# Splitting a layer's mixing weights on two compute engines instead of with chained DMAs, and moving two tiles to other PSUM banks, in a two-layer hybrid encoder

## The chip, the core and the metric

The kernel runs on one core of a Trainium2 chip. The core has five engines that this text names: TensorE (PE, matmuls; its weight loads are PEld), VectorE (DVE), ScalarE (ACT), GpSimd (POOL) and SyncE (SP), which here only issues DMAs. Each engine works through its own queue in order, and waits on semaphores for the others. The metric is the device time of one execution in microseconds (us).

## The reference

Two layers of a bidirectional encoder over 512 tokens of width 1024, in float32. Each layer mixes the tokens with attention heads and a recurrent group side by side, and then applies a gated MLP:

```python
h = rmsnorm(x, g_mix[l])
z = h @ w_in[l]                                   # 1024 x 2560
q, k, v, x_rec, gate = split(z)                   # 512 each
att = neighbourhood_attention(q, k, v, rel_bias[l])       # 8 heads of 64, 8 x 16 window
xc = depthwise_conv(x_rec, ...)
rec = (rg_lru(xc, forward) + rg_lru(xc, backward)) * gelu(gate)
x = x + concat(rmsnorm(att), rmsnorm(rec)) @ w_out[l]     # the mixing part ends here
h = rmsnorm(x, g_ffn[l])
u_act, u_lin = split(h @ w_up[l])                 # 3072 each
x = x + (gelu(depthwise_conv(u_act)) * u_lin) @ w_down[l]
```

A last rmsnorm follows the second layer.

## The kernel before

Every float32 product is made of three matmuls (mm3): each operand is split into a rounded half hi and the remainder lo, and hi*hi + hi*lo + lo*hi are accumulated in PSUM. The activations lie transposed, 128 features by 512 tokens a tile.

The weights come in chunks of 128 x 1024 (eight blocks of 128 x 128; the gates of the recurrence have chunks of 128 x 512). weight_plan lists the chunks in the order of their use, and chunk hands out the next one; at that moment it calls split_to for the chunks up to three ahead and load_to for those up to six ahead. There are four hi and four lo buffers (p_hi, p_lo) and two raw buffers (p_raw). A chunk gets its halves in one of three ways:

- The common way (lines 171 to 184 and 204 to 213): SP loads the chunk into a raw buffer, ScalarE writes the rounded hi (L210), VectorE subtracts to get lo (L211). MLP and output weights go this way in both layers, and the first four chunks of each layer.
- By DMA (by_dma, L157; L175 and lines 194 to 204), in layer 0 for the query, key, value and gate columns of w_in and for the recurrence's gates, 20 chunks in all: GpSimd issues a DMA that casts the chunk straight into hi; ScalarE copies it negated into lo (L200, ahead of its other work by urgent(1)); then GpSimd issues a second DMA that reads the chunk again and adds it to lo (L201).
- Kept (kept, L217 to L234), for the same 20 chunks of layer 1: they are split during the MLP of layer 0 and stored in DRAM, and SP loads both halves (L172).

The mixing part of a layer follows the hand-written list MIX, which is the order of PE's work as the code is written. A scheduler then places the instructions of each engine's queue; work inside urgent() comes early. The steps that matter here, for heads in pairs (block i holds heads 2i and 2i + 1): q, k, v and g are the query, key, value and gate tiles i (24 matmuls each; "a" and "b" are their halves), t are the gates of the recurrence, c its convolution, u the value's transposes to tokens, S the scores of a head with their maximum and exponentials, T the transposes of its probabilities, P the products with the values. A block reads `k1a t1a k1b P1 t1b v1a e0 S2 v1b S3 g1a u1 c3 g1b T2 q2a q2b P2 T3`. The values exist as vh and vl (L611, L612); GpSimd copies shifted parts of them into edge (L616) for the products at the window's edge. The probabilities are split into pt tiles by ScalarE (L708) and VectorE (L709), the whole part first and the edge part second.

PSUM has eight banks: three in ps_mm, two in ps_s (scores), two in ps_pt (transposed probabilities), one in ps_o. The first projection of a layer (xr, columns 12 to 15) takes the three of ps_mm and ps_o; query and key tiles take ps_mm (L575, L584).

Of the kernel before, what the change touches and what calls it, by code (L numbers as in the profile page):

```python
# [10 lines left out]
F32R = mybir.dt.float32r  # L11
AF = mybir.ActivationFunctionType
ALU = mybir.AluOpType

P = 128
# [85 lines left out]
def encoder(ctx: ExitStack, tc: tile.TileContext, x_d, w_d, cols_d, bias_d, out_d):  # L101
    nc = tc.nc
    plan = weight_plan()
# [16 lines left out]
    p_lo = pool("p_lo", 4)  # L120
# [3 lines left out]
    ps_mm = pool("ps_mm", 3, PS)  # L124
    ps_s = pool("ps_s", 2, PS)
# [6 lines left out]
    def psum(pl, name):  # L132
        return pl.tile([P, T], F32, tag="ps", name=name)
# [6 lines left out]
    def f32(ap):  # L140
        return ap.bitcast(F32)

    def urgent(level=2):
        return tc.high_priority(offset=level * URGENT) if level else ExitStack()


    raws, highs, lows, halves, kept = {}, {}, {}, {}, {}
# [1 line left out]
    AHEAD_LOAD, AHEAD_SPLIT = 6, 3  # L149

    def pieces(i):
        return (slice(0, 1024),) if i else (slice(0, 512), slice(512, 1024))

    def width(i):
        return P * len(plan[i][2])

    def by_dma(i):  # L157

        w, _, bs = plan[i]
        return w == "gate" or w == "w_in" and bs[0][1] != 12  # L160

    def load_to(n):
        while state["load"] < min(n, len(plan)):
            i = state["load"]
            if by_dma(i):
                if i > state["use"] + 3:
                    return
                highs[i] = p_hi.tile([P, 1024], F32R, tag="hi", name=f"hi{i}")
                if i in kept:
                    lows[i] = p_lo.tile([P, 1024], F32R, tag="lo", name=f"lo{i}")  # L170
                    for n, t in enumerate((highs[i], lows[i])):
                        for h in range(width(i) // 512):  # L172
                            nc.sync.dma_start(f32(t[:, 512 * h:512 * h + 512]), kept[i][n, h])
                else:
                    nc.gpsimd.dma_start(highs[i][:, :width(i)], w_d[i][:, :width(i)])  # L175
                state["load"] += 1
                continue
            raws[i] = p_raw.tile([P, 1024], F32, tag="raw", name=f"raw{i}")
            for n, sl in enumerate(pieces(i)):
                nc.sync.dma_start(raws[i][:, sl], w_d[i][:, sl])  # L180
                if i == n == 0:
                    nc.sync.dma_start(x[0], x_d[0])
            state["load"] += 1

    def split_to(n):
        while state["split"] < min(n, len(plan)):
            i = state["split"]
            if by_dma(i) and i > state["use"] + 2:
                return
            load_to(i + 1)  # L190
            if i in kept:
                halves[i] = highs.pop(i), lows.pop(i)
                state["split"] += 1
                continue
            if i in highs:
                hi = highs.pop(i)
                lo = p_lo.tile([P, 1024], F32R, tag="lo", name=f"lo{i}")
                with urgent(1):
                    ws = slice(0, width(i))
                    nc.scalar.activation(lo[:, ws], f32(hi[:, ws]), AF.Copy, scale=-1.0)  # L200
                    nc.gpsimd.dma_start(lo[:, ws], w_d[i][:, ws], accum_op=ALU.add)  # L201
                halves[i] = (hi, lo)
                state["split"] += 1
                continue
            raw = raws.pop(i)
            hi = p_hi.tile([P, 1024], F32R, tag="hi", name=f"hi{i}")
            lo = p_lo.tile([P, 1024], F32R, tag="lo", name=f"lo{i}")
            with urgent(0):
                for sl in pieces(i):
                    nc.scalar.activation(hi[:, sl], raw[:, sl], AF.Copy)  # L210
                    nc.vector.tensor_tensor(out=lo[:, sl], in0=raw[:, sl], in1=f32(hi[:, sl]), op=ALU.subtract)  # L211
            halves[i] = (hi, lo)
            state["split"] += 1

    later = [i for i in range(len(plan)) if by_dma(i) and plan[i][1] == 1]

    def split_later():  # L217

# [273 lines left out]
    def layer(l, xn):  # L492
# [79 lines left out]
        qk = {}  # L572

        def query_tile(i):
            ps = psum(ps_mm, f"qps{l}{i}")  # L575
            yield from column_parts(ps, "w_in", l, i, xg, 4)
            with urgent():
                for n in range(2):
                    rows = slice(64 * n, 64 * n + 64)
                    nc.vector.tensor_tensor(out=in_group(q_pair[rows, :, n]), in0=by_group(ps)[rows],  # L580
                                            in1=by_group(rb)[rows], op=ALU.mult)

        def key_tile(i):
            ps = psum(ps_mm, f"kps{l}{i}")  # L584
            yield from column_parts(ps, "w_in", l, 4 + i, xg, 4)
            qk[4 + i] = big(p_h, "h", f"k{l}{i}")
            with urgent():
                nc.vector.scalar_tensor_tensor(out=qk[4 + i], in0=ps, scalar=0.125, in1=rb, op0=ALU.mult, op1=ALU.mult)
# [366 lines left out]
```

## Time and profile before

| | |
|---|---|
| runs shown | 1227.52 us median (three runs, lowest 1226.66, one of them 2701.48) |
| profiled execution | 1226.75 us, of which 1224.0 us lie between its first and its last instruction (span) |
| PE busy | 1198.3 us, 98% |
| VectorE busy | 736.7 us, 60% |
| ScalarE busy | 503.7 us, 41% |
| GpSimd busy | 123.7 us, 10% |
| DMA | 161.29 MB, 132 GB/s over the span |

The mixing part of layer 0 fills about the first 200 us, its MLP the time to about 610 us; then layer 1 does the same. The profile's engine times are shares of the span. A row of a timeline gives start and duration in us, engine, line, operation, output and inputs; the bracket at its end is the time that the engine stood idle before it, and what it waited for. Matmul rows overlap, as they are pipelined: their pace is read from the distances of their starts.

### The profile page before, as it was taken

The page shows a single profiled execution, that of the slowest core. Times are in us where ns is not written, and L with a number is a line of the kernel's source. Part 1 is how long each engine was busy: PE and PEld are TensorE (multiplying, and loading weights), DVE is VectorE, ACT ScalarE, POOL GpSimd, SP SyncE. Part 2 cuts the span into 40 slices and gives each one's busy share as a digit, 9 for nine tenths or more (in the row PEclk, how much of TensorE's full clock was granted, in tenths as well). Part 3 has the DMA queues.
Part 4 walks back from the last instruction along what each step waited for, and adds up shares of the span by engine and source line. Part 5 has one row for each costly group of instructions (what it writes and reads, how often), then busy time and mean ns, then how long its engine had stood idle before and what let it go on. Part 6 is the DMA issues. An engine that isn't in the chain of part 4 may idle for free.

```text
span 1224.0 us, 14611 instructions
## 1 busy us (share of the span) xinstructions
PE 1198.3 (98%) x5566; PEld 999.0 (82%) x5566; DVE 736.7 (60%) x1217; ACT 503.7 (41%) x741; POOL 123.7 (10%) x206
## 2 busy tenths in 40 slices
PE   9888999999999999999999999999999999999997
PEld 7777788888888888888888888888888888888886
DVE  6476684877653376662736777677556255555454
ACT  5566783544332144332416667443322212323220
POOL 3222210022220022210000100100000000000000
PEclk9999999999999999999999999999999999999999
DMA  8656632366663366653245443142232332322322
GB/s 270 142 133 124 140 104 70 103 206 213 229 217 99 102 216 224 215 171 103 92 132 191 141 148 104 38 136 90 100 104 88 101 103 86 104 93 96 103 69 69
DMA packets 53942, 161.29 MB, mean 132 GB/s; under 512 B 6768, under 2 KB 9968, under 8 KB 53872
## 3 DMA queue, kind: packets, MB, share of 16 engines
q1 hardware_dynamic: 39328, 113.17, 28.3%
q0 software_dynamic: 14400, 47.20, 14.1%
q8 instruction: 43, 0.70, 0.2%
q14 instruction: 27, 0.22, 0.1%
q10 hardware_dynamic: 144, 0.00, 0.0%
HBM read 139.37 MB, written 20.97 MB: 131 GB/s over the span
## 4 chain that ended last, share of the span: by engine, by line
PE 90%; DVE 4%; issue 3%; DMA 1%; POOL 1%; ACT 1%; POOLq 0%; DVEq 0%; ACTq 0%
PE dn L248 7%; PE dn L250 7%; PE dn L249 7%; PE pa L248 7%; PE pl L248 7%; PE pa L249 7%; PE pl L249 7%; PE pl L250 7%; PE pa L250 7%; PE out L250 2%; PE out L248 2%; PE out L249 2%; DMA hi<-in_w 1%; PE up L248 1%; PE up L250 1%
## 5 line engine op out<-in xcount | busy, mean ns | idle before, releaser
L210 ACT ACTIVATE hi<-raw 128x1024 fp32r<-128x1024 f32 (+1 forms) x169 | 178.3, 1055 | 388.3 <-PE dn L249 160.5
L211 DVE TENSOR_TENSOR lo<-raw,hi 128x1024 fp32r<-128x1024 f32 (+1 forms) x169 | 205.3, 1215 | 133.5 <-ACT hi L210 132.7
L818 DVE TENSOR_TENSOR ua<-pa,g_ffn_rb 128x512 f32<-128x512 f32 x44 | 30.4, 692 | 113.7 <-PE pa L250 113.7
L826 ACT ACTIVATE uc<-uc,cols 128x512 f32<-128x512 f32 x48 | 34.8, 724 | 115.9 <-DVE uc L824 115.9
L827 DVE TENSOR_TENSOR uc<-pl,uc 128x512 f32<-128x512 f32 x44 | 30.3, 689 | 44.6 <-PE pl L250 43.8
L466 POOL TENSOR_TENSOR fin_r<-fin_ms,expo 128x2 f32<-128x2 f32 x2 | 1.4, 697 | 377.7 <-DVE fin_ms L464 377.7
L795 DVE TENSOR_TENSOR dns<-dn,g_ffn_rb 128x512 f32<-128x512 f32 x30 | 20.5, 689 | 29.4 <-PE dn L250 29.4
L233 POOL DMA_DIRECT2D kept<-lhi x36 | 19.5, 543 | 177.8 <-ACT lhi L227 174.5
L824 DVE SCALAR_TENSOR_TENSOR uc<-ua,cols,uc 128x511 f32<-128x511 f32 x48 | 36.0, 750 | 1.5
L822 DVE SCALAR_TENSOR_TENSOR uc<-ua,cols,uc 128x511 f32<-128x511 f32 x48 | 35.7, 744 | 0.1
L200 ACT ACTIVATE lo<-hi 128x1024 fp32r<-128x1024 f32 (+1 forms) x20 | 19.4, 972 | 32.7 <-DMA hi<-in_w 24.6
L228 DVE TENSOR_TENSOR llo<-lraw,lhi 128x512 fp32r<-128x512 f32 x36 | 24.7, 687 | 10.7 <-ACT lhi L227 10.7
L682 ACT ACTIVATE prob<-prob,mx 128x192 f32<-128x192 f32 (+1 forms) x64 | 27.5, 430 | 1.1 <-DVE mx L680 0.9
L248 PE MATMUL out<-atth,hi 128*128 128x512 f32 x64 | 25.7, 402 | 0.0
L249 PE MATMUL out<-attl,hi 128*128 128x512 f32 x64 | 25.2, 394 | 0.0
L201 POOL DMA_DIRECT2D lo<-in_w x20 | 17.5, 877 | 75.8 <-ACT lo L200 75.8
L250 PE MATMUL out<-atth,lo 128*128 128x512 f32 x64 | 25.2, 393 | 0.0
L616 POOL CAST edge<-vh 64x384 fp32r<-64x384 f32 x16 | 10.1, 629 | 144.3 <-ACT vh L611 143.8
L233 POOL DMA_DIRECT2D kept<-llo x36 | 19.5, 543 | 48.9 <-DVE llo L228 46.3
L821 DVE TENSOR_SCALAR uc<-ua,cols 128x512 f32<-128x512 f32 x48 | 23.4, 487 | 1.6
L667 PE MATMUL s<-k,q_pair 128*128 128x192 f32 (+1 forms) x128 | 22.0, 314 | 2.4 <-DVE mx L675 2.4
L556 DVE SCALAR_TENSOR_TENSOR ti<-ti,xc 128x512 f32<-128x512 f32 x16 | 11.0, 689 | 21.9 <-ACT ti L548 21.9
(934 smaller groups left out, 3687.2 us busy)
## 6 DMA issues: line engine op xcount, KB each, us to landing
raw<-in_w SPq DMA_DIRECT2D x167, 512.0 KB, 3.5
lraw<-in_w POOLq DMA_DIRECT2D x36, 256.0 KB, 4.2
kept<-lhi POOLq DMA_DIRECT2D x36, 256.0 KB, 2.5
kept<-llo POOLq DMA_DIRECT2D x36, 256.0 KB, 3.0
hi<-kept SPq DMA_DIRECT2D x36, 256.0 KB, 2.8
lo<-kept SPq DMA_DIRECT2D x36, 256.0 KB, 4.0
hi<-in_w POOLq DMA_DIRECT2D x16, 512.0 KB, 5.4
lo<-in_w POOLq DMA_DIRECT2D x16, 512.0 KB, 5.6
```

The costliest lines, as they stand in the source:

```text
L210: nc.scalar.activation(hi[:, sl], raw[:, sl], AF.Copy)
L211: nc.vector.tensor_tensor(out=lo[:, sl], in0=raw[:, sl], in1=f32(hi[:, sl]), op=ALU.subtract)
L233: nc.gpsimd.dma_start(d, f32(parts[h][n]))
L248: nc.tensor.matmul(ps, a[0], b[0], start=start, stop=False)
L249: nc.tensor.matmul(ps, a[0], b[1], start=False, stop=False)
L250: nc.tensor.matmul(ps, a[1], b[0], start=False, stop=stop)
L682: nc.scalar.activation(pr[b], pr[b], AF.Exp, bias=mx[:, b % 4:b % 4 + 1], accum_out=sm[:, b % 4:b % 4 + 1])
L818: nc.vector.tensor_tensor(out=ua, in0=pa, in1=rbf[0], op=ALU.mult)
L822: nc.vector.scalar_tensor_tensor(out=c[:, 1:], in0=ua[:, :T - 1], scalar=w[0], in1=c[:, 1:], op0=ALU.mult, op1=ALU.add)
L824: nc.vector.scalar_tensor_tensor(out=c[:, :T - 1], in0=ua[:, 1:], scalar=w[2], in1=c[:, :T - 1], op0=ALU.mult, op1=ALU.add)
L826: nc.scalar.activation(c, c, AF.Gelu_apprx_tanh, bias=col("conv_ffn_b", j, l))
L827: nc.vector.tensor_tensor(out=c, in0=pl_, in1=c, op=ALU.mult)
```

## The change

The 20 chunks of layer 0 that came by DMA now go the common way: by_dma becomes is_kept, which holds for layer 1 alone, and the branches with L175 and L200 to L201 are gone. pieces takes the width of the chunk, as the gates' chunks are 512 wide. The kept chunks of layer 1 are handled as before. Beside that, the query tile 0 and the key tile 0 of each layer take their PSUM bank from ps_s, all others from ps_mm as before.

```diff
     def pieces(i):
-        return (slice(0, 1024),) if i else (slice(0, 512), slice(512, 1024))
+        return (slice(0, width(i)),) if i else (slice(0, 512), slice(512, 1024))
...
-    def by_dma(i):
-
-        w, _, bs = plan[i]
-        return w == "gate" or w == "w_in" and bs[0][1] != 12
+    def is_kept(i):
+
+        w, l, bs = plan[i]
+        return l == 1 and (w == "gate" or w == "w_in" and bs[0][1] != 12)
...
-            if by_dma(i):
+            if is_kept(i):
                 if i > state["use"] + 3:
                     return
                 highs[i] = p_hi.tile([P, 1024], F32R, tag="hi", name=f"hi{i}")
-                if i in kept:
-                    lows[i] = p_lo.tile([P, 1024], F32R, tag="lo", name=f"lo{i}")
-                    for n, t in enumerate((highs[i], lows[i])):
...
-                else:
-                    nc.gpsimd.dma_start(highs[i][:, :width(i)], w_d[i][:, :width(i)])
+                lows[i] = p_lo.tile([P, 1024], F32R, tag="lo", name=f"lo{i}")
+                for n, t in enumerate((highs[i], lows[i])):
...
-            if by_dma(i) and i > state["use"] + 2:
+            if is_kept(i) and i > state["use"] + 2:
                 return
...
-            if i in highs:
-                hi = highs.pop(i)
-                lo = p_lo.tile([P, 1024], F32R, tag="lo", name=f"lo{i}")
-                with urgent(1):
-                    ws = slice(0, width(i))
-                    nc.scalar.activation(lo[:, ws], f32(hi[:, ws]), AF.Copy, scale=-1.0)
-                    nc.gpsimd.dma_start(lo[:, ws], w_d[i][:, ws], accum_op=ALU.add)
-                halves[i] = (hi, lo)
-                state["split"] += 1
-                continue
...
         def query_tile(i):
-            ps = psum(ps_mm, f"qps{l}{i}")
+            ps = psum(ps_mm if i else ps_s, f"qps{l}{i}")
...
         def key_tile(i):
-            ps = psum(ps_mm, f"kps{l}{i}")
+            ps = psum(ps_mm if i else ps_s, f"kps{l}{i}")
```

The change moves instructions at several places of the queues. The line numbers of the changed kernel are 13 lower in the parts that follow the removed code; numbers behind tile names are the program's own.

PE in layer 0, around the transposes of head 1 (ptw, pte) and the products of head 0 (o), before; kps is the key tile 1:

```order
L248 MATMUL o_719<-pt_679,vh_648 128x256
L249 MATMUL o_719<-pt_680,vh_648 128x256
L250 MATMUL o_719<-pt_679,vl_649 128x256
L248 MATMUL o_719<-pt_681,edge_161 128x256
L249 MATMUL o_719<-pt_682,edge_161 128x256
L250 MATMUL o_719<-pt_681,edge_162 128x256
L699 MATMUL ptw_735<-ident,prob_160 128x128 x4
L703 MATMUL pte_736<-ident,prob_160 128x128 x3
L248 MATMUL kps_761<-xg_g_mix_0h,hi_542 128x512
```

The same place of the changed kernel:

```order
L237 MATMUL qps_700<-xg_g_mix_7h,lo_486 128x512
L686 MATMUL ptw_749<-ident,prob_160 128x128 x4
L690 MATMUL pte_750<-ident,prob_160 128x128 x3
L235 MATMUL kps_775<-xg_g_mix_0h,hi_550 128x512
L236 MATMUL kps_775<-xg_g_mix_0l,hi_550 128x512
L237 MATMUL kps_775<-xg_g_mix_0h,lo_551 128x512
L235 MATMUL kps_775<-xg_g_mix_1h,hi_550 128x512
L236 MATMUL kps_775<-xg_g_mix_1l,hi_550 128x512
L237 MATMUL kps_775<-xg_g_mix_1h,lo_551 128x512
L235 MATMUL o_733<-pt_692,vh_661 128x256
L236 MATMUL o_733<-pt_693,vh_661 128x256
L235 MATMUL kps_775<-xg_g_mix_2h,hi_550 128x512
```

The twelve products of head 0 stood ahead of head 1's transposes; now they stand behind them and behind six of the key tile's matmuls, two more of which lie among them. It is the only place at which PE's order differs.

VectorE in layer 0, second block, from the last scaling of head 3's probabilities on, before (vl is the value tile's lower half, xc the convolution):

```order
L686 TENSOR_SCALAR prob_160<-prob_160,sm_924 128x128
L612 TENSOR_TENSOR vl_969<-vtp_963,vh_968 128x512
L709 TENSOR_TENSOR pt_1009<-ptw_999,pt_1008 128x512
L520 TENSOR_SCALAR xc_3_976<-xrs_3_414,cols 128x512
L709 TENSOR_TENSOR pt_1011<-pte_1000,pt_1010 128x384
L523 SCALAR_TENSOR_TENSOR xc_3_976<-xrs_3_414,cols,xc_3_976 128x510
```

The same place of the changed kernel (lo_964 is the lower half of a gate chunk, lo_1036 of the value chunk 2):

```order
L673 TENSOR_SCALAR prob_160<-prob_160,sm_941 128x128
L599 TENSOR_TENSOR vl_987<-vtp_981,vh_986 128x512
L696 TENSOR_TENSOR pt_1027<-ptw_1017,pt_1026 128x512
L198 TENSOR_TENSOR lo_964<-raw_884,hi_963 128x512
L507 TENSOR_SCALAR xc_3_994<-xrs_3_422,cols 128x512
L198 TENSOR_TENSOR lo_1036<-raw_967,hi_1035 128x1024
L696 TENSOR_TENSOR pt_1029<-pte_1018,pt_1028 128x384
```

Two of the 20 added subtractions stand ahead of the second half of the probabilities' split. The other blocks have them at similar places.

ScalarE in layer 0, second block, around the recurrence's square root (L560, w) and the exponentials (L682, prob), before:

```order
L682 ACTIVATE prob_159,sm_888<-prob_159,mx_887 128x192 x3
L554 ACTIVATE a_852<-a_849 128x512
L376 ACTIVATE rec_acc<-fb_533 128x512
L200 ACTIVATE lo_1017<-hi_949 128x512
L560 ACT_TABLE_LOAD
L560 ACTIVATE w_784<-w_784 128x1024
L682 ACT_TABLE_LOAD
L682 ACTIVATE prob_160,sm_924<-prob_160,mx_923 128x192 x3
```

The same place of the changed kernel (the square root is L547, the exponentials are L669):

```order
L197 ACTIVATE hi_880<-raw_798 128x1024
L539 ACTIVATE w_800<-w_800,sp 128x512
L541 ACTIVATE a_868<-a_865 128x512
L363 ACTIVATE rec_acc<-fb_544 128x512
L547 ACT_TABLE_LOAD
L547 ACTIVATE w_800<-w_800 128x1024
L669 ACT_TABLE_LOAD
L669 ACTIVATE prob_159,sm_905<-prob_159,mx_904 128x128
L669 ACTIVATE prob_159,sm_905<-prob_159,mx_904 128x192 x3
L669 ACTIVATE prob_160,sm_941<-prob_160,mx_940 128x192 x3
```

The negated copy ahead of the square root is gone, a rounding copy stands further ahead, and the exponentials of both heads now come behind the square root.

## Rows read from the trace of the kernel before

**Rows 1.** Page, part 1: busy us, share of the span and instructions of each engine.

```profile
PE 1198.3 (98%) x5566; PEld 999.0 (82%) x5566; DVE 736.7 (60%) x1217; ACT 503.7 (41%) x741; POOL 123.7 (10%) x206
```

**Rows 2.** Timeline of PE at four places: start us, duration us, engine, line, operation, count.

```profile
25.93 0.65 PE L399 MATMUL g_mix_rps<-ident,g_mix_r 128*128 128x128 f32 x4
...
241.92 0.95 PE L387 MATMUL fcps<-ones,g_ffn_acc 128*128 128x1 f32 x8
...
638.71 0.60 PE L399 MATMUL g_mix_rps<-ident,g_mix_r 128*128 128x128 f32 x4
...
834.53 0.95 PE L387 MATMUL fcps<-ones,g_ffn_acc 128*128 128x1 f32 x8
```

**Rows 3.** Table by stage: stretch, its us, busy us (instructions) of each engine, PEclk, DMA, GB/s.

```profile
core 0: us, PE busy (x) PEld busy (x) DVE busy (x) ACT busy (x) POOL busy (x), PEclk, DMA share, GB/s
29.00:180.00 151.00, 136.23 (x665) 113.14 (x664) 101.16 (x237) 103.43 (x181) 35.98 (x51) 0.98 0.57 128
642.00:775.00 133.00, 132.15 (x675) 112.03 (x673) 102.08 (x239) 90.05 (x166) 9.70 (x16) 1.00 0.43 142
```

**Rows 4.** The same table, two slices of layer 0; PEclk is the mean granted clock.

```profile
60.00:80.00 20.00, 16.28 (x73) 12.95 (x73) 17.85 (x39) 11.03 (x27) 4.94 (x9) 0.91 0.58 136
100.00:120.00 20.00, 16.71 (x78) 13.85 (x77) 14.89 (x26) 14.08 (x24) 6.52 (x9) 0.91 0.46 95
```

**Rows 5.** Chain of waits in layer 0: start us, duration us, what.

```profile
64.78 5.57 DMA hi<-in_w
70.37 1.06 ACT lo L200
...
71.72 0.86 POOL lo L201
```

**Rows 6.** Waits of ScalarE, layer 0: engine, line, releaser: us in total, times, longest.

```profile
ACT lo L200 <- DMA hi<-in_w: 24.6, 10, 6.1
```

**Rows 7.** Timeline of ScalarE, VectorE and PE in the second block of layer 0.

```profile
100.43 0.64 ACT L200 ACTIVATE lo<-hi 128x512 fp32r<-128x512 f32 x1 [4.66 <-issue]
...
103.47 0.69 DVE L562 TENSOR_TENSOR ti<-ti,w 128x512 f32<-128x512 f32 x1 [5.94 <-ACT w L560]
...
110.84 0.39 PE L249 MATMUL o<-pt,vh 128*128 128x256 f32 x1 [2.87 <-ACT lo L200]
```

**Rows 8.** Waits of PE, layer 0, the longest and the split's.

```profile
PE o L249 <- ACT lo L200: 4.8, 2, 2.9
PE o L248 <- ACT vh L611: 2.8, 1, 2.8
PE s L667 <- DVE mx L675: 2.4, 1, 2.4
PE qps L248 <- DVE xrs L515: 1.5, 1, 1.5
...
PE o L249 <- DVE pt L709: 0.9, 2, 0.5
```

**Rows 9.** Tile hi in layer 0: operation, count, duration ns min/median/max, starts, forms.

```profile
L200 ACT ACTIVATE lo<-hi x20: 622/1056/1066, 20.1 to 152.5; 128x1024 fp32r<-128x1024 f32 x16, 128x512 fp32r<-128x512 f32 x4
L210 ACT ACTIVATE hi<-raw x11: 629/1049/1062, 3.7 to 198.5; 128x1024 fp32r<-128x1024 f32 x9, 128x512 fp32r<-128x512 f32 x2
L211 DVE TENSOR_TENSOR lo<-raw,hi x9: 691/1217/1226, 4.3 to 178.5; 128x1024 fp32r<-128x1024 f32 x7, 128x512 fp32r<-128x512 f32 x2
```

**Rows 10.** Timeline of ScalarE, VectorE and PE in the second block of layer 1.

```profile
694.45 1.06 ACT L560 ACTIVATE w<-w 128x1024 f32<-128x1024 f32 x1
...
696.68 0.69 DVE L562 TENSOR_TENSOR ti<-ti,w 128x512 f32<-128x512 f32 x1
...
705.27 0.55 DVE L709 TENSOR_TENSOR pt<-pte,pt 128x384 fp32r<-128x384 f32 x1
...
708.91 0.28 PE L249 MATMUL o<-pt,edge 128*128 128x128 f32 x1
```

**Rows 11.** Timeline of PE: first query tile, second matmul, and the one 23 starts later.

```profile
31.17 0.40 PE L249 MATMUL qps<-xg_g_mix_0l,hi 128*128 128x512 f32 x1
...
36.40 0.39 PE L248 MATMUL kps<-xg_g_mix_0h,hi 128*128 128x512 f32 x1
```

**Rows 12.** Page, part 6, and line L180 in layer 0: loads into raw, issue to landing.

```profile
raw<-in_w SPq DMA_DIRECT2D x167, 512.0 KB, 3.5
...
DMA to landing us min/median/max: 2.9/4.5/6.4
```

**Rows 13.** Line L616 in the whole trace: edge copies, ns min/median/max.

```profile
L616 POOL CAST edge<-vl x16: 502/507/1367, 73.7 to 770.0; 64x384 fp32r<-64x384 f32 x16
```

More of the change, by code (lines that the diff above doesn't have):

```diff
@@ L168, in load_to @@
                 highs[i] = p_hi.tile([P, 1024], F32R, tag="hi", name=f"hi{i}")
-                if i in kept:
-                    lows[i] = p_lo.tile([P, 1024], F32R, tag="lo", name=f"lo{i}")
-                    for n, t in enumerate((highs[i], lows[i])):
-                        for h in range(width(i) // 512):
-                            nc.sync.dma_start(f32(t[:, 512 * h:512 * h + 512]), kept[i][n, h])
-                else:
-                    nc.gpsimd.dma_start(highs[i][:, :width(i)], w_d[i][:, :width(i)])
+                lows[i] = p_lo.tile([P, 1024], F32R, tag="lo", name=f"lo{i}")
+                for n, t in enumerate((highs[i], lows[i])):
+                    for h in range(width(i) // 512):
+                        nc.sync.dma_start(f32(t[:, 512 * h:512 * h + 512]), kept[i][n, h])
                 state["load"] += 1
@@ L213, in split_to @@
             state["split"] += 1
-    later = [i for i in range(len(plan)) if by_dma(i) and plan[i][1] == 1]
+    later = [i for i in range(len(plan)) if is_kept(i)]
     def split_later():
```

## The prediction

> **What bounds the kernel now.** I read the busy line of the page first: TensorE (PE) is busy 98% of the 1224.0 us, so a change pays only where PE waits or runs at the lower clock [rows 1]. The next question is where that is. The two layers do the same matmuls, so their mixing stages can be laid side by side, from the transposes of g_mix_rps (ahead of the last eighth of the first projection) to the column sums fcps in the MLP's first projection. Layer 0 takes 241.92 - 25.93 = 215.99 us, layer 1 takes 834.53 - 638.71 = 195.82 us [rows 2]. The difference, **20.17 us**, is what layer 0 pays for having its weights prepared on the way, since layer 1 reads halves that were prepared during layer 0's MLP.
>
> The reader should see three parts in it. In the stage table PE is idle 151.00 - 136.23 = 14.77 us in layer 0 and 0.85 us in layer 1 [rows 3]. In two slices of 20 us the granted clock is 0.91 of full [rows 4]; a mean of 0.91 between the levels 1.0 and 0.5 (2.4 and 1.2 GHz) is 3.6 us at the low level, so 1.8 us lost in each, 3.6 us together, and in both slices PE had just stood still for more than 2 us. The rest, 20.17 - 13.92 - 3.6 = 2.65 us, is restarts and waits too short to be listed.
>
> Why PE waits is in the next two views. The chain of waits runs through the chained DMAs: a transfer into hi (5.57 us), ScalarE's negated copy into lo (1.06), then the issue of the adding transfer on GpSimd (0.86) [rows 5]. These copies hold ScalarE's queue: it stood idle 24.6 us in front of ten of them for a transfer [rows 6]. What stands behind pays: in the second block lo_1017 begins at 100.43 after 4.66 us of idleness, only then come the square root and the exponentials, VectorE takes up the scan's factors at 103.47 after 5.94 us of nothing, and PE stops for 2.87 us in front of the probabilities' product at 110.84 [rows 7]. In the list of PE's waits the largest entries are the products (4.8, 2.8), the scores (2.4) and the first query tile (1.5) [rows 8].
>
> **The change part by part.** *Removed:* on GpSimd 40 DMA issues (20 L175, 20 L201); on ScalarE 20 negated copies; from memory one of two reads of each chunk. *Added:* on ScalarE 20 rounding copies of the same shapes at 1.05 us instead of 1.056 for the wide form, so nothing net; on SP 20 loads; on VectorE 20 subtractions, 16 wide at 1.22 us and 4 narrow at 0.69: 19.5 + 2.8 = 22.3 us [rows 9].
>
> *What is gained.* The new copies need no transfer after them, and a load runs ahead into the raw ring instead of starting when a hi buffer comes free. So I take the whole 20.17 us as the amount at stake and subtract what I find still waiting. The floor: profiled time 1226.75 - 20.17 = **1206.6 us** (the span is 1224.0, with 2.75 us around it; the median of the runs shown, 1227.52, is 0.77 above).
>
> *Bank edit.* PE's first query tile waited 1.5 us for VectorE to empty a bank of the first projection [rows 8]. In the scores' pool the banks are idle then; that wait goes. Its price is nothing as long as the scores come later than the evacuation of the first key tile, and they must, since they read its result. Were that cover gone, it would be one evacuation of 0.69 us, as a narrow VectorE operation takes [rows 9].
>
> *VectorE's load.* In layer 1's stretch of 133 us VectorE is busy 102.08 [rows 3]. Some 17 of the 20 subtractions fall into the same stretch of layer 0: 14 x 1.22 + 3 x 0.69 = 19.2, so 121 of 133 us. That fits, with 12 us to spare, but VectorE is in order, so position counts. In the second block two of them (lo_964, lo_1036) stand ahead of the edge half of the probabilities' split. In layer 1 that split ends at 705.27 + 0.55 = 705.82 and PE needs it at 708.91: 3.09 us of slack [rows 10]. The two add 0.69 + 1.22 = 1.91. ScalarE's two copies (2.1 us) ahead of the square root do not add to it in full, since in layer 1 VectorE takes up the factors 1.2 us after the square root's end (694.45 + 1.06 against 696.68) [rows 10]. So no wait, or a short one: I put 0.5 us for the three later blocks together.
>
> *First block.* Here PE's order moves: the first products come behind the second transposes and six key matmuls. The way from the end of the first transposes on PE to these products is 24 query matmuls, the transposes and 6 matmuls. 23 steps take 36.40 - 31.17 = 5.23 us, 0.227 each [rows 11], so 30 x 0.227 + 0.8 (an estimate for seven transposes: half of seven such steps) = 7.6 us. The other way, from the same point: the split of the probabilities and the narrow lo_630 on VectorE, some 3 us (five operations of about 0.6, by pt and lo) [rows 9, 10]; that frees the raw buffer, so the next load can go, 3.5 us by the median of all wide loads [rows 12]; then hi_776 on ScalarE, 1.05, and behind it in the queue the value's rounding copy, 0.63 by the narrow form. Together 8.2 us, 0.6 late. Four edge copies on GpSimd (0.51 each [rows 13]) end 2.0 us after the value's copy, and PE has about five steps (1.1 us) of other work before it needs the last: 0.6 + 2.0 - 1.1 = 1.5 us in all. With the load at 2.9 or 6.4 us [rows 12] it is 0.9 or 4.4.
>
> *GpSimd's copies.* Four edge copies sit on that path. Their median is 0.507 us, the longest 1.367 [rows 13], so they can stretch by 0.86. The Trainium skill (GPSIMD Engine Reference, 1. Specifications) says that GpSimd's SBUF interfaces are shared with VectorE and contend with instructions that have two SBUF inputs; the new subtractions are such; by that rule the longest row would be the usual one and the sum would be 3.4 us higher. The trace shows the spread but not its cause, so the median stays in the sum, and the long row is a rival (C).
>
> *Others.* Two subtractions (2.4 us) stand ahead of the first scores' maximum; I let 0.5 of them through to the first transposes. ScalarE's copy g_mix_rb stands behind the copies of three chunks: 0.5 for the first ten microseconds after the projection. Both are choices between 0 and 1. Clock: one fall (1.8) at even odds, 0.9. Sum: 0.5 + 1.5 + 0.5 + 0.5 + 0.9 = 3.9; less 0.65, most of the 0.85 that layer 1 pays too and that is in the floor already, 3.25. Forecast: 1206.6 + 3.25 = 1209.85, **1210 us**. Ends of the unknown terms: 0 and 4.4 for the first products, 0 and 1.8 for the clock, 0 and 1 for each of the three others, which gives 1206.6 to 1206.6 + 4.4 + 1.8 + 3 - 0.65 = 1215.2.
>
> **Rivals.** (A) *VectorE becomes the one that PE waits for.* For it: 121 of 133 us; against it: 1.91 added against 3.09 of slack. If the products' waits in the second and third block (4.8 and 0.9 [rows 8]) come back, and the other half of the clock's fall with them, the time is 1210 + 5.7 + 0.9 = 1216.6. Chance 0.20.
> (B) *Layer 0 becomes like layer 1:* 1206.6. For it: less traffic, so loads at 2.9. Chance 0.15.
> (C) *Edge copies stretch* beside the subtractions: 4 x 0.86 = 3.4 more, 1213.4; the products of later blocks have slack. Chance 0.08.
> (D) *Slower: the ring of two raw buffers.* A load can't be issued before the subtraction two chunks ahead, which stands in VectorE's queue behind the softmax; meanwhile hi stands in ScalarE's queue ahead of work that the softmax needs. If each block paid one full trip, 6.4 + 1.05 + 1.22 = 8.7 us, and a clock fall of 1.8, it is 4 x 10.5 = 41.9 on the floor: 1248.5. It decides from 20.17 / 4 = 5.0 us a block. Against it: only in the first block does a copy that waits for such a load stand ahead of the value's copy. Chance 0.05.
> (E) *It does nothing:* the waits are of the softmax chain itself, whoever splits the weights: 1227. Against it: layer 1 has the same chain and waits 0.85. Chance 0.06.
>
> **How the numbers follow.** The forecast has 0.46, with a range of its own of 1207.5 to 1213. The range 1205.5 to 1219 takes in A, B and C (0.89 in all) and leaves out D and E. Over 2% faster would need 24.5 us, more than the stage has to give: 0.02. Over 2% slower, beyond 1252, only in a worse form of D: 0.02. Within 2%, about what a measurement of this kernel can tell from no change: 0.96.
>
> **What would show it.** Right: no ScalarE wait for a weight transfer; the stage of layer 0 at 196 to 201 us; the list of PE's waits without the first query tile and the 2.87; the clock at 1.0 from the second block on. The remaining wait should be at the first products, released by the value's copy or the edge copies. Wrong: PE's waits at the second and third blocks released by VectorE's split (A), loads that land late with hi behind them (D), or a stage that still takes 216 us (E).

## The result and the profile after

The changed kernel takes **1209.95 us** (median of four runs, 1209.74 to 1210.03) against 1227.09 us for the kernel before, run beside it: a ratio of 0.9863, 95% interval 0.9844 to 0.9882. The forecast was 1210.0 us with a range of 1205.5 to 1219. The total is right, but some of what leads to it was not foreseen, so it has to be taken apart.

The busy line of the page [rows 1 before]: PE keeps its work, VectorE has 20 us more, GpSimd 29 us less. One of two reads of each chunk has gone (DMA 151.85 MB after 161.29).

```profile
PE 1192.5 (99%) x5566; PEld 996.3 (82%) x5566; DVE 757.0 (63%) x1237; ACT 502.3 (42%) x741; POOL 95.1 (8%) x166
```

The four markers on PE's timeline [rows 2 before]; columns: start us, duration us, engine, line, operation, count (of the matmuls in the stretch that was asked for).

```profile
25.57 0.49 PE L386 MATMUL g_mix_rps<-ident,g_mix_r 128*128 128x128 f32 x3
...
223.44 0.95 PE L374 MATMUL fcps<-ones,g_ffn_acc 128*128 128x1 f32 x8
...
620.22 0.38 PE L386 MATMUL g_mix_rps<-ident,g_mix_r 128*128 128x128 f32 x2
...
815.97 0.95 PE L374 MATMUL fcps<-ones,g_ffn_acc 128*128 128x1 f32 x8
```

Layer 0's mixing stage takes 223.44 - 25.57 = 197.87 us, where it took 215.99: 18.12 less. Layer 1's takes 195.75 (195.82 before), the MLP between them 396.78 (396.79). The last transposes on PE (fin_rps) start 382.36 us behind the last marker in both kernels, at 1216.89 before and at 1198.33 after. So up to there the whole effect is in layer 0's mixing stage (and 0.36 us ahead of it). Behind there something is lost: from that start to the end of the span it is 7.11 us in the kernel before (span 1224.0) and 9.67 in the changed one (1208.0). The spans are given to 0.1 us, so these two figures, and what lies around the span, are good to 0.05.

| | before | after | difference |
|---|---|---|---|
| to the first marker | 25.93 | 25.57 | -0.36 |
| layer 0's mixing stage | 215.99 | 197.87 | -18.12 |
| MLP, layer 1, MLP, to fin_rps | 974.97 | 974.89 | -0.08 |
| fin_rps to the end of the span (the tail below) | 7.11 | 9.67 | +2.56 |
| around the span | 2.75 | 1.74 | -1.01 |
| profiled execution | 1226.75 | 1209.74 | -17.01 |

The table by stage [rows 3 and 4 before]: stretch, its us, busy us (instructions) of each engine, PEclk, DMA share, GB/s. In layer 0 PE is idle 2.20 us of 133, in layer 1 0.84; the clock is at 1.00 in the two slices in which it had been 0.91.

```profile
29.00:162.00 133.00, 130.80 (x665) 110.18 (x664) 118.10 (x256) 101.05 (x180) 10.80 (x16) 1.00 0.26 82
623.50:756.50 133.00, 132.16 (x675) 112.12 (x674) 102.11 (x239) 90.03 (x166) 9.70 (x16) 1.00 0.44 142
...
60.00:80.00 20.00, 18.38 (x96) 15.11 (x95) 18.18 (x27) 12.22 (x20) 2.98 (x4) 1.00 0.28 88
100.00:120.00 20.00, 20.00 (x103) 17.11 (x102) 18.02 (x41) 17.28 (x28) 0.00 (x0) 1.00 0.24 77
```

PE's waits between layer 0's two markers are now these three lines (what waits, for whom: us in total, times, longest), where [rows 8] had 4.8, 2.8, 2.4 and 1.5:

```profile
PE o L237 <- POOL edge L603: 1.0, 2, 0.5
PE o L235 <- ACT vh L598: 0.6, 1, 0.6
PE ptw L686 <- DVE prob L673: 0.2, 1, 0.2
```

The first two are the first block's products. The timelines of ScalarE, GpSimd, VectorE and PE there (the bracket is idleness before, and the releaser):

```profile
63.95 1.06 ACT L197 ACTIVATE hi<-raw 128x1024 fp32r<-128x1024 f32 x1 [0.45 <-DMA raw<-in_w]
64.92 0.58 ACT L598 ACTIVATE vh<-vtp 128x512 fp32r<-128x512 f32 x1
...
65.56 1.07 POOL L603 CAST edge<-vh 64x384 fp32r<-64x384 f32 x2 [41.33 <-ACT vh L598]
66.68 2.03 POOL L603 CAST edge<-vl 64x384 fp32r<-64x384 f32 x2
...
66.83 1.51 DVE L198 TENSOR_TENSOR lo<-raw,hi 128x1024 fp32r<-128x1024 f32 x1
...
65.55 0.38 PE L235 MATMUL o<-pt,vh 128*128 128x256 f32 x1 [0.65 <-ACT vh L598]
67.32 0.33 PE L237 MATMUL o<-pt,edge 128*128 128x128 f32 x1 [0.49 <-POOL edge L603]
68.76 0.39 PE L237 MATMUL o<-pt,edge 128*128 128x256 f32 x1 [0.49 <-POOL edge L603]
```

This is the chain of the forecast: a load lands, hi, the value's copy, the edge copies, the products. PE waits 0.65 + 0.49 + 0.49 = 1.63 us in it; 1.5 had been put. One thing stands out: the two edge copies of vl take 2.03 us where those of vh just ahead take 1.07, and VectorE's lo beside them takes 1.51 where its median was 1.217 [rows 9].

ScalarE still waits for transfers:

```profile
ACT hi L197 <- DMA raw<-in_w: 12.4, 6, 3.1
```

Three of these six (2.60, 1.62 and 2.12 us, from 186 us on) are for the output weights, and the kernel before has the same three at its L210 (2.47, 1.49 and 2.23 us). For the chunks that the change moved, three waits are left, 0.45, 2.54 and 3.06 us (63.95, 97.99 and 129.80), where [rows 6] has ten of 24.6 in all: a quarter.

**The tail.** The last instruction of GpSimd's queue that takes time is one that the profile calls DRAIN; its record begins just ahead of the last power (fin_r, 0.70 us on GpSimd from 1197.58) and takes it in. Here are the instructions of the program's closing line on GpSimd in the last microseconds (count, duration in ns min/median/max, first and last start in us), and SP's waits at that line, first of the kernel before:

```profile
L950 POOLq DRAIN  x1: 4984/4984/4984, 1216.1 to 1216.1; - x1
...
SPq L950 <- PEq L950: 0.7, 2, 0.5
```

and of the changed kernel:

```profile
L937 POOLq DRAIN  x1: 9639/9639/9639, 1197.5 to 1197.5; - x1
...
SPq L937 <- PEq L937: 3.1, 2, 2.6
```

Before, the drain ended at 1221.1 and lay hidden behind the outputs' transfers. After, it takes 9.64 us, ends at 1207.2, and the outputs are done 2.6 us earlier: SP, and with it the program's end, waits. The view puts SP's wait down to PE's sequencer (PEq); that it is GpSimd's drain is read from the times (1204.7 + 2.6 = 1207.3) and tested below. No term of the forecast speaks of it. Why it is longer in a kernel in which GpSimd issues 40 transfers less (148 before: the 40 of layer 0 and 108 that load and store the kept chunks; 108 after) was the first question for the experiments.

### The profile page after: what moved, and what is told of

Its sections match the earlier page's. It is cut to its first block, busy times and chain, and to the rows that moved or that the text cites. A ratio compares the mean times of both kernels' runs of the same rounds, so it can differ in the third digit from the quotient of the medians.

```text
span 1208.0 us, 14574 instructions
## 1 busy us (share of the span) xinstructions
PE 1192.5 (99%) x5566; PEld 996.3 (82%) x5566; DVE 757.0 (63%) x1237; ACT 502.3 (42%) x741; POOL 95.1 (8%) x166
## 2 busy tenths in 40 slices
DMA packets 51061, 151.85 MB, mean 126 GB/s; under 512 B 6448, under 2 KB 9648, under 8 KB 50992
## 4 chain that ended last, share of the span: by engine, by line
PE 94%; DVE 4%; issue 1%; POOL 0%; DMA 0%; ACT 0%; POOLq 0%; DVEq 0%; SPq 0%; ACTq 0%
PE dn L237 7%; PE dn L235 7%; PE dn L236 7%; PE pl L237 7%; PE pa L237 7%; PE pa L235 7%; PE pl L235 7%; PE pl L236 7%; PE pa L236 7%; PE out L237 2%; PE out L235 2%; PE out L236 2%; PE xr L235 1%; PE up L235 1%; PE vps L237 1%; PE vps L235 1%
## 5 line engine op out<-in xcount | busy, mean ns | idle before, releaser
L197 ACT ACTIVATE hi<-raw 128x1024 fp32r<-128x1024 f32 (+1 forms) x189 | 197.5, 1046 | 399.3 <-PE dn L236 160.5
L198 DVE TENSOR_TENSOR lo<-raw,hi 128x1024 fp32r<-128x1024 f32 (+1 forms) x189 | 228.0, 1206 | 133.5 <-ACT hi L197 132.4
L669 ACT ACTIVATE prob<-prob,mx 128x192 f32<-128x192 f32 (+1 forms) x64 | 27.4, 430 | 1.1 <-DVE mx L667 0.9
L214 ACT ACTIVATE lhi<-lraw 128x512 fp32r<-128x512 f32 x36 | 22.1, 616 | 0.0
L654 PEld LDWEIGHTS s<-k,q_pair 128*128 128x128 f32 x128 | 20.8, 190 | 1.2
L783 DVE TENSOR_TENSOR x<-x,dns 128x512 f32<-128x512 f32 x30 | 20.1, 688 | 0.4
```

Of the source, the lines that this page charges most:

```text
L654: nc.tensor.matmul(ps[:, o:o + ROWS * w], q_pair[:, b], kt[:, kc0 // 8:(kc0 + w) // 8], start=True, stop=True)
```

## The experiments

The kernel before, run beside each group, took 1226.98, 1225.79 and 1226.49 us. The kernels with one raw buffer, with subtractions twice and with more transfers or memsets were run once each, the others four to ten times; stage, tail and drain are of one profiled execution each. "Stage" is layer 0's mixing stage between the two markers, "tail" the time from the start of fin_rps to the end of the span, "drain" the GpSimd instruction above.

| kernel | time, us | stage | tail | drain, ns |
|---|---|---|---|---|
| before | 1227.09 | 215.99 | 7.11 | 4984 |
| changed | 1209.95 | 197.87 | 9.67 | 9639 |
| split alone (e_split_only) | 1210.10 | 198.1 | 9.6 | 9639 |
| bank edit alone (e_bank_only) | 1226.69 | 218.3 | 7.5 | 4986 |
| negation on GpSimd (e_neg_pool) | 1247.89 | 235.4 | 7.4 | 4986 |
| one raw buffer (e_raw1) | 1340.54 | 214.9 | 9.7 | 9642 |
| subtractions twice (e_dve2) | 1217.48 | 205.3 | 9.6 | 9646 |
| 40 transfers more (e_dma40) | 1208.22 | 197.8 | 7.1 | 4247 |
| 20 transfers more (e_dma20) | 1206.78 | 197.9 | 6.9 | 2616 |
| 40 memsets more (e_mem40) | 1210.31 | 197.8 | 9.6 | 9646 |
| power off GpSimd (e_finr_act) | 1207.18 | 197.8 | 7.0 | 10922, at 817 us |
| edge copies on ScalarE (e_edge_act) | 1208.71 | 196.7 | 9.7 | 9642 |
| changed, again (e_again) | 1209.90 | 197.9 | 9.6 | 9639 |
| both mends (e_both) | 1205.98 | 196.6 | 6.9 | 10921, at 816 us |

### Each half of the change alone

The changed kernel without the bank edit:

```diff
-            ps = psum(ps_mm if i else ps_s, f"qps{l}{i}")
+            ps = psum(ps_mm, f"qps{l}{i}")
...
-            ps = psum(ps_mm if i else ps_s, f"kps{l}{i}")
+            ps = psum(ps_mm, f"kps{l}{i}")
```

> The changed kernel with the bank edit undone: the first query and key tile take the projection's banks again, the split stays on ScalarE and VectorE. If the bank edit was worth what the prediction said (a PE wait of 1.5 us at the first query tile), this kernel takes 1210.0 + 0.5 to 1.5 = 1210.5 to 1211.5 us and the wait is in PE's list again, layer 0's mixing stage 198.4 to 199.4 us. Rival: the first block's products wait for their transfer all the same and absorb it, so the stage stays at 197.9 and the time at 1210.0. On the tail: it issues 108 transfers on GpSimd as the changed kernel does; if their number sets the length of GpSimd's last drain, the drain is 9.6 us again and the tail after PE's last transposes 9.7; if the length is a matter of chance from run to run, it can be anything.

The kernel before with these two lines as in the changed kernel:

> The kernel before with the bank edit alone. If the 20 us in layer 0 come from the chained transfers, nearly all of them stay: 1227.1 - 1.5 = 1225.6 us at best, layer 0's stage 214.5 to 216 us, the wait at the first query tile gone. Rival (the bank edit is a large part of the gain): below 1220. On the tail: 148 transfers on GpSimd as in the kernel before; if their number sets GpSimd's last drain, it is 5.0 us and the tail 7.1.

The split alone takes 1210.10 us (ratio 0.9856, 0.9838 to 0.9875): all of the gain. The bank edit alone takes 1226.69 (ratio 0.9997, 0.9986 to 1.0007): none of it that can be told from noise, as the interval goes from 1.7 us less to 0.9 us more. Without the bank edit the first query tile's wait should have come back. It doesn't; the time is the one that the rival named, but not by its reason, as there is no such wait to absorb. The reason is in the first microseconds of the stage. ScalarE in the kernel before, and, below the dots, in the kernel with the split alone:

```profile
28.93 0.63 ACT L200 ACTIVATE lo<-hi 128x512 fp32r<-128x512 f32 x1 [5.32 <-DMA hi<-in_w]
29.47 0.58 ACT L401 ACTIVATE g_mix_rb<-g_mix_rps 128x512 f32<-128x512 f32 x1
...
26.89 0.60 ACT L388 ACTIVATE g_mix_rb<-g_mix_rps 128x512 f32<-128x512 f32 x1 [1.48 <-PE g_mix_rps L386]
```

The norm's factors (g_mix_rb) stood behind a negated copy that waited 5.32 us for its transfer. VectorE needs them to empty the projection's banks, and the query tile needs such a bank: its 1.5 us [rows 8] came from ScalarE's queue too: the bank was late because the factors were. In the split kernel the factors are copied at once (26.89, 0.64 us after the transposes start), and the bank is free in time. In the kernel with the bank edit alone the copy stands where it stood, the query tile no longer waits, and other waits grow behind it. ScalarE there, and four lines of PE's waits:

```profile
29.43 0.63 ACT L200 ACTIVATE lo<-hi 128x512 fp32r<-128x512 f32 x1 [6.34 <-DMA hi<-in_w]
...
PE o L249 <- ACT lo L200: 4.1, 2, 2.2
PE s L667 <- DVE mx L675: 2.9, 1, 2.9
PE o L248 <- ACT vh L611: 2.7, 1, 2.7
PE gp L248 <- ACT xcs_0h L364: 1.1, 1, 1.1
```

The gates' first matmuls (gp) wait 1.1, and the scores 2.9 instead of 2.4: in this execution the wait that was taken off PE turns up again behind it. One execution doesn't show more than that. (Its stage, 218.3 us, is 2.3 longer than that of the kernel before, with a granted clock of 0.94 from 29 to 180 us where [rows 3] has 0.98; over all runs the two times are the same.)

### Who holds the wait

In the kernel before, the chain of work up to the products of the second block runs through a negated copy, the square root, the scan's factors and the split of the probabilities (start us, duration us, what; cut):

```profile
98.52 1.91 issue
100.43 0.64 ACT lo L200
...
102.38 1.07 ACT w L560
103.47 1.29 DVE ti L562 x2
...
111.24 0.48 DVE pt L709
111.76 0.33 PE o L249
```

The 4.66 us in front of that copy [rows 7] have no releaser in the profile ("issue") and are not among the 24.6 us of [rows 6]. That they too were a wait for its transfer comes out of the DMA view: the only narrow transfer into hi that GpSimd issued between 80 and 105 us went out at 94.19 and landed 6.2 us later, at 100.4. To test whether it is ScalarE's queue that matters, the copy is given to GpSimd:

```diff
-                    nc.scalar.activation(lo[:, ws], f32(hi[:, ws]), AF.Copy, scale=-1.0)
+                    nc.gpsimd.tensor_scalar(out=lo[:, ws], in0=f32(hi[:, ws]), scalar1=-1.0, scalar2=None, op0=ALU.mult)
```

> The kernel before with the negated copy into lo taken from ScalarE and given to GpSimd; the two transfers stay chained. Theory 1, ScalarE's queue: what cost the time was that ten of the copies stood in ScalarE's queue for a transfer (24.6 us) with the square root and the exponentials behind them. Then the 2.87 us wait in the second block and the idle 5.94 us of VectorE go, and the stage falls from 216.0 to 200 to 208 us, the time to 1212 to 1220. Theory 2, the chain's own length: the halves come too late whoever negates, and the copy is no faster on GpSimd, whose queue is now held in the same way, with the edge copies in it: the stage stays at 214 to 222 us, the time at 1225 to 1233.

It takes 1247.89 us (ratio 1.0156, 1.0129 to 1.0183), worse than either theory said, so it doesn't tell them apart as meant. PE's waits in layer 0's stage show why:

```profile
PE o L248 <- POOL edge L616: 11.7, 2, 9.1
PE gate L250 <- DMA lo<-in_w: 7.4, 3, 2.7
PE qps L250 <- DMA lo<-in_w: 7.0, 2, 3.5
```

ScalarE's waits for the chain are gone; but the wait for the transfer now holds GpSimd's queue, in which the edge copies stand (11.7 us). The first line is the same effect in another queue, and a GpSimd power for the norm is late by it as well (PE waits 3.1 us for it ahead of the first marker's transposes). The other two are theory 2 in part: a narrow copy takes 1.48 us on GpSimd instead of 0.63, and with it the halves themselves come too late, which in the kernel before no listed wait shows. That an in-order queue that waits for a transfer makes what stands behind it late is seen in both kernels; how the 18 us divide between the queue and the chain's length is not settled by this run. For the queue speaks that in the kernel before none of the listed waits of PE between the two markers, 14.6 us in all, is released by a transfer. The split itself changes three things about ScalarE's copies at once: the loads are issued ahead by SP, each chunk is read once instead of twice, and the copies are no longer urgent, so they stand elsewhere in the queue. No run separates the three.

### The ring of raw buffers

```diff
-    p_raw = pool("p_raw", 2)
+    p_raw = pool("p_raw", 1)
```

> The changed kernel with one raw buffer instead of two, everywhere. By rival D the ring of raw buffers is what layer 0 hangs on: with one, each chunk pays load, copy and subtraction in a row (about 3.5 + 1.05 + 1.22 = 5.8 us), and the mixing stage of layer 0 grows by 20 us or more, to 218 or beyond, with a clock fall. By the forecast's reading (loads are ahead except in the first block) each block's first chunk is late by one load of 3.5 us at the most: 198 + 4 x 3.5 = 212 us at most, the time 1213 to 1225, plus what the multilayer perceptrons pay.

The stage takes 214.9 us, 17.0 more than with two buffers and between the two expectations: more than the 14 of late loads, less than the 20 of rival D. On the mean of four blocks it is 4.3 us each, below the 5.0 at which D would have decided; a fall of the clock is in it (0.97 from 75 to 125 us). Nearly all the rest of the 131 us lies in the MLPs (from fcps of layer 0 to the next marker 459.8 us instead of 396.8), where every chunk goes through the ring. So D's mechanism is real with one buffer, and two are enough here.

### How much room VectorE has

```diff
                     nc.vector.tensor_tensor(out=lo[:, sl], in0=raw[:, sl], in1=f32(hi[:, sl]), op=ALU.subtract)
+                    if plan[i][1] == 0 and (plan[i][0] == "gate" or plan[i][0] == "w_in" and plan[i][2][0][1] != 12):
+                        nc.vector.tensor_tensor(out=lo[:, sl], in0=raw[:, sl], in1=f32(hi[:, sl]), op=ALU.subtract)
```

> The changed kernel with each of layer 0's 20 new subtractions done twice: VectorE has 22.3 us more, 19 of them in the stretch of 133 us in which it is busy 118 already, so 137 of 133. If rival A's mechanism is real and only its size was short, VectorE becomes the engine that PE waits for: waits released by VectorE at scores, probabilities and products in the second and third block, the stage of layer 0 at 203 to 212 us instead of 197.9, the time 1215 to 1225. Rival: VectorE's work in the block can slide into the projection behind it, and the slack is larger than counted: the stage stays below 201 us, the time below 1213.

The stage takes 205.3 us, 7.5 more, and the time 1217.48. PE's two longest waits in it are released by VectorE:

```profile
PE o L238 <- DVE pt L698: 3.0, 3, 2.1
PE vps L237 <- DVE k L577: 2.0, 2, 1.3
```

The first of them is the split of the probabilities, the place that rival A named. VectorE is busy 130.9 of the 133 us from 29 to 162, so it has no room left, and the clock falls once (0.95 from 140 to 175 us). So the first 22 us of subtractions cost PE 0.24 us at most, a wait that layer 1 has too (0.2), and a second 22 us cost 7.5: A was the right mechanism to fear. That the slack of 3.09 us [rows 10] takes the 1.91 us that the change adds ahead of that split, but not twice as much, fits this; with VectorE full, the run doesn't tell position from load.

### What sets the last drain

40 transfers of a small tile put back on GpSimd, and in another kernel 40 memsets at the same places; the third has 20 of the transfers:

```diff
-        for step in MIX:
+        for n_step, step in enumerate(MIX):
             what, n = step[0], int(step[1:2] or 0)
+            if l == 0 and n_step < 40:
+                d = p_kept.tile([P, 64], F32, tag=f"spare{n_step}", name=f"spare{n_step}")
+                nc.gpsimd.dma_start(d, ones[:, 0:64])
```

> The changed kernel with 40 small transfers added on GpSimd in layer 0's mixing stage (64 columns of ones to DRAM that nothing reads), so that GpSimd issues 148 transfers as in the kernel before. Theory 1: the number of GpSimd's transfers sets the length of its last drain; then the drain is 5.0 us again instead of 9.6, and the tail from PE's last transposes to the end 7.1 instead of 9.7. Theory 2: it is not the transfers (the place of the instructions in memory, the time since the last one, chance): the drain stays at 9.6. The time itself stays within 1207 to 1213 us.

> The changed kernel with 40 memsets of 16 columns added on GpSimd at the same places, in place of the transfers: 40 instructions more, no transfer more. Theory 1 (number of transfers): the drain stays at 9.6 us. Theory 3 (number or place of GpSimd's instructions): it falls to about 5.0. The time stays within 1207 to 1213 us.

> The changed kernel with 20 small transfers added on GpSimd instead of 40, so 128 of them. If GpSimd's last drain falls steadily with the number of its transfers (9.64 us at 108, 4.25 at 148), it takes 6.9 us here and is just hidden behind the outputs (tail 7.1 to 7.3). If the number counts in steps, or by what is left over in some ring, the drain is 9.6 or 4.2, or longer than either.

GpSimd's drain in the three (which program line closes a kernel depends on its length), 40 transfers, 40 memsets, 20 transfers:

```profile
L940 POOLq DRAIN  x3: 45/102/4247, 1198.2 to 1205.9; - x3
...
L940 POOLq DRAIN  x3: 40/102/9646, 1197.9 to 1208.0; - x3
...
L940 POOLq DRAIN  x3: 45/102/2616, 1197.3 to 1204.7; - x3
```

It is the transfers and not the instructions: with 40 memsets the drain stays at 9.65, with 40 transfers it is 4.25, the tail 7.1 again, and the kernel is faster with more work in it. But a length that falls steadily with the number is ruled out: with 128 transfers the drain is 2.62, shorter than with 108 (9.64) and with 148 (4.25 and 4.98), which neither half of the last expectation gave as its value. In the table it is the same to 10 ns in all six programs with 108 transfers that end in it, so it is no chance of a run; 128 transfers, and 148 with small ones, were seen once each. What is counted, and why 40 small transfers and 40 large ones differ by 0.7 us, stays open.

### Two mends

The last power off GpSimd, so that its drain starts earlier:

```diff
-            nc.vector.tensor_scalar(out=ms, in0=cps[:, 0:2], scalar1=1.0 / D, scalar2=EPS, op0=ALU.mult, op1=ALU.add)
+            nc.scalar.activation(ms, cps[:, 0:2], AF.Sqrt, scale=1.0 / D, bias=eps)
             r = p_s.tile([P, 2], F32, tag="rr", name=f"fin_r{th}")
-            nc.gpsimd.tensor_tensor(out=r, in0=ms, in1=expo[:, 0:2], op=ALU.pow)
+            nc.vector.reciprocal(r, ms)
```

> The changed kernel with the last power (fin_r, both halves) taken from GpSimd: ScalarE's square root and VectorE's reciprocal instead. GpSimd is then done long before the end, and its drain lies beside the last products. If the drain is what ends the span (it ended at 1207.2 of 1208.0), the end falls to that of the outputs, 1204.7 and about 0.8 behind it: span 1205.5, time 1207.5 (1206.8 to 1208.5). Rival: the drain's length is only a record, and the program ends by something else: no change, 1210. Rival: the square root's table has to be loaded on the last path, 1.3 us or so: 1209.

It takes 1207.18 us (1206.75 to 1207.79). The drain is longer, 10.92 us, and costs nothing, since it starts with GpSimd's last power, now that of layer 1's second norm, 388 us before the end; SP no longer waits for it:

```profile
L937 POOLq DRAIN  x3: 40/102/10922, 817.1 to 1204.8; - x3
...
SPq L937 <- PEq L937: 0.7, 2, 0.5
```

So the drain did end the program, and the tail of 9.67 us is explained by it; why the drain is that long is not. The square root's table is loaded once, for the first half (1.28 us at 1186.68), and not on the last path.

Two of the four edge copies of the first block on ScalarE:

```diff
-                        nc.gpsimd.tensor_copy(e[rows, dst], src[rows, cs])
+                        if l == i == 0 and src is lo:
+                            nc.scalar.activation(e[rows, dst], src[rows, cs], AF.Copy)
+                        else:
+                            nc.gpsimd.tensor_copy(e[rows, dst], src[rows, cs])
```

> The changed kernel with two of the first block's four edge copies (those of vl) on ScalarE, which is idle there, instead of GpSimd. If GpSimd's and VectorE's work slow each other there (rival C: vl's copies 2.03 us for two instead of 1.02, VectorE's lo beside them 1.51 instead of 1.22), the two waits of 0.49 us for edge copies in front of the products go, VectorE's lo takes 1.22 to 1.25, and the time falls by 0.5 to 1.0 us, to 1209.0 to 1209.5. If the copies are late only because the value's copy is, the waits stay at half or more, and the time at 1209.7 to 1210.2.

It takes 1208.71 us (1208.34 to 1208.94), the stage 196.7 us. VectorE and ScalarE at the place shown above:

```profile
66.86 1.21 DVE L198 TENSOR_TENSOR lo<-raw,hi 128x1024 fp32r<-128x1024 f32 x1
...
66.29 1.07 ACT L604 ACTIVATE edge<-vl 64x384 fp32r<-64x384 f32 x2 [0.76 <-DVE vl L599]
```

VectorE's lo takes 1.21 us again, the two copies 1.07, and both waits for edge copies are gone from PE's list; the wait for the value's copy (0.65) stays. VectorE's next instruction (L510 at 67.99) takes 0.74 us instead of 0.99 as well. That is the mechanism of rival C, but the 1.2 us are not all its price: the last of vl's copies ends 1.35 us earlier, 0.96 of it because the two are shorter, and 0.39 because they no longer stand behind those of vh in one queue (66.29 against 66.68).

Both mends together, beside the changed kernel:

> The changed kernel once more, as the measure for the next one on the same chip: 1210.0 us (1209.5 to 1210.5), GpSimd's last drain 9.64 us and a tail of 9.7 if they belong to the program and not to the run.

> The changed kernel with both mends: the last power off GpSimd (ScalarE's square root, VectorE's reciprocal) and two of the first block's edge copies on ScalarE. If the two gains are of different places they add: about 2.8 us and 1.2 us, so 4.0 below the changed kernel: 1206.0 us (1205.5 to 1206.5), layer 0's stage 196.7 us, tail 7.0 us. Rival: the transposes at the end fall into the low clock in one and not in the other, and half a microsecond of the gain goes: 1206.5 to 1207.

With both mends the kernel takes 1205.98 us (1205.56 to 1206.43) against 1209.90: 3.92 us less, the sum of the two gains as forecast. Its ratio to the kernel before is 0.9831 (0.9818 to 0.9844). It beats both kernels.

## Why the prediction was right, and where it was not

**The amount at stake.** Right. The stage of layer 0 fell to within 2.12 us of layer 1's (197.87 against 195.75); the split alone brings it. The gain of 18.12 us is 1.2 more than the 20.17 - 3.25 = 16.9 that the sum left.

**Bank edit.** The wait went, as said, but the cause was wrong. The step read the 1.5 us as a lack of banks; they came from ScalarE's queue, by way of the factors, and go with the split alone. The edit alone brings nothing that can be measured, and its absence costs nothing (1210.10 against 1209.95). It should have been followed one releaser further back: bank, VectorE, ScalarE, transfer.

**VectorE's load.** Right: 0.24 us of waits in the later blocks, 0.5 were put. Rival A did not come about, and the doubled subtractions show a load at which it does.

**First block.** Right in chain: 1.63 us, 1.5 were put, released by the value's copy and the edge copies as named. The value's copy was late by 0.65 us, 0.6 were put. The size of the rest is luck in part: the edge copies ended 3.2 us after the value's copy (2.0 were put), and PE had 2.2 us of other work in that time (1.1 were put); the two errors cancel, which leaves 0.98 where 0.9 had been put.

**GpSimd's copies (C).** The rival came about in part. The pair of vl copies takes 2.03 us beside a subtraction, 1.07 without; the subtraction itself takes 1.51 instead of 1.22. Two of four copies were hit, and the price was 1.2 us at most, not the 3.4 of all four at the longest row. The Trainium skill (GPSIMD Engine Reference, 1. Specifications) says that GpSimd's SBUF interfaces are shared with VectorE and contend with instructions that have two SBUF inputs. The trace agrees: moved to ScalarE, the copies take 1.07 us beside the same subtraction, and the subtraction 1.21.

**Clock, first transposes, first ten microseconds.** 0.9 + 0.5 + 0.5 us had been put, as even odds and choices; none came. The granted clock is 1.00 throughout the stage, and the longest listed wait of PE in it is 0.65 us.

**ScalarE's waits.** "No ScalarE wait for a weight transfer" was wrong: 6.05 us in three remain for these chunks. Only the one in the first block, 0.45 us, stands on PE's path; behind the other two (97.99 and 129.80) PE has no listed wait until 155.71. With one raw buffer less, ScalarE's waits for transfers between the markers rise to 48.7 us in 18, and the stage grows by 17.0.

**The missing term.** Nothing was said of the end of the program. Of the 18.56 us by which PE's last transposes came early, 2.56 were lost in the last drain. The edit is 1000 us away from it, and GpSimd was busy for only 10% of the span; but the edit takes 40 transfers from GpSimd, and the drain depends on them. The forecast came out at 1210 because the stage gave 1.2 and the start 0.36 us more than was put, and because the profiled execution of before had 2.75 us around its span, where the changed kernel has 1.74: together 2.6, about as much as the tail lost. A total that agrees to 0.1 us is here no proof of the sum.

## What to carry to other kernels

A copy that waits for a DMA on an in-order engine is paid for by whatever stands behind it in that queue; read what the releaser itself waited for, one step further back, before putting a wait down to a lack of buffers. Giving the same wait to another engine's queue moves the price, and can raise it. After a change at the start of a program, compare the last ten microseconds of the two traces too: the closing instructions of an engine that hardly works can end the program, and work that is taken off that engine's last stretch may be worth more than a stage's last wait.

## What the runs showed of the hardware that was not expected

GpSimd's last DRAIN is long and depends on the transfers that GpSimd has issued: 9.64 us after 108 of them, 2.62 after 128, 4.25 after 148 of which 40 are small, 4.98 after 148 large ones, and 10.92 after 108 where it follows GpSimd's power at 817 us, so the number of transfers isn't all that sets it. 40 memsets instead of transfers don't change it. Where it follows the last power at the end, what goes beyond some 7 us is on the path (it starts at 1197.5, the outputs are done at 1204.7).

In the first block GpSimd's copies and a VectorE subtraction beside them slow each other: 2.03 instead of 1.07 us for two copies, 1.51 instead of 1.21 for the subtraction; the same two copies on ScalarE take 1.07 and leave the subtraction as it is.
